# The last attention pair's steps ahead of the output gate, and half of the gate between that pair's keys and queries

## The chip, the cores and the metric

One core of one Trainium2 chip runs the kernel. The metric is the device time of one execution in microseconds, the median of three runs. Engines are named as in the profile: PE (matmul), PEld (its weight load), DVE, ACT, POOL, and SP, which here only issues DMAs.

## What is computed

One layer on 1024 tokens of width 1024, in float32. The reference, cut to what matters here:

```python
xn = rms_norm(h, attn_norm[l])
u = xn @ w_in[l]
o_a = hgrn2_mixer(u[..., o0:o1], u[..., o1:o2], u[..., o2:o3], u[..., o3:o4], lb_all[l], hg_norm[l])
o_b = fox_mixer(u[..., o4:o5], u[..., o5:o6], u[..., o6:o7], u[..., o7:IN_COLS], fox_f_bias[l], fox_norm[l])
h = h + jnp.concatenate([o_a, o_b], axis=-1) @ w_out[l]
h = h + hier_moe(rms_norm(h, ffn_norm[l]), w_group[l], b_group[l], w_expert[l], b_expert[l],
                 w_gate[l], w_up[l], w_down[l])
```

`hgrn2_mixer` is a gated recurrence over four heads of 128. Its fourth argument is the output gate: the recurrence's result is multiplied by silu of it. `fox_mixer` is causal softmax attention over eight heads of 64, with a forget bias. `hier_moe` sends every token to two of 16 experts.

## The kernel before

Each float32 operand of a large matmul is held as a rounded part (`hi`) and a remainder (`lo`), and a product is three matmuls in a row (`mm3`, lines 249 to 251). `piece` (line 168) loads one piece of a weight matrix by a DMA of SP, rounds it on ACT (line 178) and forms the remainder on DVE (line 179). The rounded pieces have three buffers.

The first half of the program is a list of calls (lines 575 to 600), one for each projection and mixer:

- `hg_fq(h)` projects forget gate and query of recurrence head h; `hg_core(h)` runs the head. Its scores are a chain of seven rounds: 16 small matmuls (line 504) into one PSUM bank (`hc`), a masked copy on DVE (lines 507 and 517), products into the query tile on DVE (lines 508 and 521) and into the key tile on POOL (line 522), then the next round. Two halves of state and output follow (lines 531 to 566).
- `fox_kq(p)` projects keys and queries of a pair of attention heads. The results leave PSUM (two banks `bk`) through ACT and DVE (lines 304 to 312) and are copied to the other 64 partitions by DMAs of SP (`mv`, line 293). Each of the two projections is 48 matmuls of 512 columns.
- `fox_core(p)` runs the pair in steps (`fox_steps`, line 352). `row` makes the logits of one block of 128 queries for one head on PE (lines 379 to 383), adds the bias and takes the minimum on DVE (line 384) and the exponential on ACT (line 388). `attend` takes two finished rows piece by piece: up to four transposes on PE (line 401), rounding on ACT (`ph`, line 406), remainder on DVE (`pl`, line 407), and matmuls with the values into one bank (`ub`, lines 411 and 412). For block pair I of 0 to 3 and either head it has I+1 pieces. `collect` copies the bank out (line 432), transposes it (line 435) and sums (line 437); after I = 1 and I = 3 `finish` normalizes and stores. The logits' tiles have four buffers.
- `hg_g(p)` projects half of the output gate: 8 token tiles of 24 matmuls of 256 columns, so 192 matmuls, each tile leaving through ACT and DVE (lines 571 and 572) and a DMA into `g_d` (line 573).

No engine's order is written out by hand. The build's scheduler places every instruction; calls that come earlier in the program go first, and later work fills in where an earlier call has nothing ready.

At the end of this half the program before mixes calls by hand. The last pair's steps are made with `steps = fox_steps(3)`: 18 of them come between `hg_g(0)` and `hg_g(1)`, and the others between the roundings of the output matrix's eight rows (`prep`, line 619: a cast on ACT at line 621, a subtraction on POOL or, for rows 2 and 5, on DVE at line 622), the first two token tiles' inputs of the output projection (`front_a`, line 629: a product with the gate on DVE at line 636, eight transposes at line 642, lines 645 and 646) and the first tile's output projection (`front_parts(0)`, line 655, 48 matmuls of 512 columns). `tc.issue_after` holds a cast of `prep` behind the latest rounding of `attend`, and a part of the projection behind the latest transposes:

```python
    def prep(k, lim=True):
        with (tc.issue_after(LF['act'].ins) if lim else nullcontext()):
            A.copy(WOH[k], raws[k])
        (G, V)[k in (2, 5)].tensor_sub(WOL[k], raws[k], WOH[k].bitcast(F32))
```

After it come the other seven tiles of the output projection with routing, and then the experts, which the change leaves alone.

Of the kernel before, what the change touches and what calls it, by code (L numbers as in the profile page):

```python
# [80 lines left out]
def build(ctx, tc, x, attn_norm, w_in, hg_lb_logits, hg_norm, fox_f_bias, fox_norm, w_out, ffn_norm,  # L81
          w_group, b_group, w_expert, b_expert, w_gate, w_up, w_down, final_norm, cf, ci, cl0, out, dbg=None):
    nc = tc.nc
    V, A, G, T = nc.vector, nc.scalar, nc.gpsimd, nc.tensor
# [12 lines left out]
    def bank():  # L97
        return ps.tile([128, 512], F32, name="bk", tag="bk", bufs=NB["bk"])
# [58 lines left out]
    def rtile(name):  # L157
        return up.tile([128, S], F32R, name=name, tag="u", bufs=NU)
# [9 lines left out]
    def piece(ks, c0, n, extra=None, raw=None):  # L168
        m = ks.stop - ks.start
        raw = wp.tile([128, m, n], F32, name="wraw", tag="wraw", bufs=1) if raw is None else raw  # L170
        hi = wp.tile([128, m, n], F32R, name="whi", tag="whi", bufs=3)
        lo = wp.tile([128, m, n], F32R, name="wlo", tag="wlo", bufs=3)
        if extra is None:
            nc.sync.dma_start(raw, w_in_v[:, ks, c0:c0 + n])
        else:
            nc.sync.dma_start(raw[:, :, 0:n - 8], w_in_v[:, ks, c0:c0 + n - 8])
            nc.sync.dma_start(raw[:, :, n - 8:n], w_in_v[:, ks, extra:extra + 8])
        A.copy(hi, raw)  # L178
        V.tensor_sub(lo, raw, hi.bitcast(F32))  # L179
        return hi, lo  # L180
# [67 lines left out]
    def mm3(o, l, r, first, last):  # L248
        T.matmul(o, l[0], r[0], start=first, stop=False)  # L249
        T.matmul(o, l[0], r[1], start=False, stop=False)  # L250
        T.matmul(o, l[1], r[0], start=False, stop=last)  # L251

    def proj_c(c0, evac):
        hi, lo = piece(slice(0, KD), c0, 128)
        for th in range(2):
            b = bank()
            t = slice(th * 512, th * 512 + 512)
            for k in range(KD):
                mm3(b, (hi[:, k], lo[:, k]), (XH[th][:, k], XL[th][:, k]), k == 0, k == KD - 1)
            evac(b, t)  # L260

    def proj_t(c0, n, evac, extra=None, pc=None):
        pc = pc or [piece(slice(4 * g, 4 * g + 4), c0, n, extra) for g in range(2)]
        for i in range(NT):
            b = bank()
            t = slice(i % 4 * 128, i % 4 * 128 + 128)
            for k in range(KD):
                hi, lo = pc[k // 4]
                mm3(b[:, :n], (XH[i // 4][:, k, t], XL[i // 4][:, k, t]), (hi[:, k % 4], lo[:, k % 4]), k == 0, k == KD - 1)
            evac(b, i)  # L270
# [22 lines left out]
    def mv(d, o):  # L293
        nc.sync.dma_start(d.bitcast(F32), o.bitcast(F32))

    def fox_kq(p):
        ka, kb, qa, qb, ql, qm = (rtile(n) for n in ("ka", "kb", "qa", "qb", "ql", "qm"))
        kl = up.tile([128, S], F32R, name="kl", tag="L", bufs=4)

        lo_, up_ = slice(0, 64), slice(64, 128)  # L300

        def ev_k(b, sl):
            for hi, h, o in ((ka, lo_, up_), (kb, up_, lo_)):
                A.copy(hi[h, sl], b[h])
                V.tensor_sub(kl[h, sl], b[h], hi[h, sl].bitcast(F32))  # L305
                mv(hi[o, sl], kl[h, sl])

        def ev_q(b, sl):
            for hi, lo, h, o in ((qa, ql, lo_, up_), (qb, qm, up_, lo_)):
                A.activation(hi[h, sl], b[h], AF.Copy, scale=-0.125)  # L310
                mv(hi[o, sl], hi[h, sl])
                V.scalar_tensor_tensor(lo[h, sl], b[h], -0.125, hi[h, sl].bitcast(F32), op0=OP.mult, op1=OP.subtract)
                mv(lo[o, sl], lo[h, sl])
        proj_c(2560 + 128 * p, ev_k)
        proj_c(2048 + 128 * p, ev_q)
        out = (((qa, ka), (ql, ka)), ((qb, kb), (qm, kb)))
        FS[p] = out
# [32 lines left out]
    LF = {}  # L350
# [107 lines left out]
    def fox_core(p):  # L458
        for _ in fox_steps(p):
            pass  # L460
# [13 lines left out]
    def hg_fq(h):  # L474
        F, K, Q = utile("hF"), utile("hK"), utile("hQ")
        HF[h], HK[h], HQ[h] = F, K, Q

        def ev_f(b, sl):
            A.activation(F[:, sl], b, AF.Tanh, scale=0.5)
            G.tensor_scalar(F[:, sl], F[:, sl], lb[:, 1, h:h + 1], lb[:, 0, h:h + 1], op0=OP.mult, op1=OP.add)  # L480
            G.tensor_scalar(K[:, sl], F[:, sl], -0.5, 0.5, op0=OP.mult, op1=OP.add)

        def ev_q(b, sl):
            A.activation(Q[:, sl], b, AF.Tanh, scale=0.5)
            V.scalar_tensor_tensor(Q[:, sl], Q[:, sl], 1.0, b, op0=OP.add, op1=OP.mult)

        proj_c(512 + 128 * h, ev_f)
        proj_c(128 * h, ev_q)
# [79 lines left out]
    def hg_g(p):  # L568
        def ev(b, i):
            z = up.tile([128, 256], F32, name="sg", tag="sg", bufs=2)  # L570
            A.activation(z, b[:, 0:256], AF.Tanh, scale=0.5)
            V.scalar_tensor_tensor(z, z, 1.0, b[:, 0:256], op0=OP.add, op1=OP.mult)
            nc.sync.dma_start(g_d[i * 128:(i + 1) * 128, 256 * p:256 * p + 256], z)
        proj_t(1536 + 256 * p, 256, ev)
# [4 lines left out]
    fox_v(0)  # L579
    fox_gate()  # L580
    fox_kq(0)
    fox_core(0)
    hg_fq(1)
    hg_core(1)
    hg_fq(2)
    fox_kq(1)
    fox_core(1)
    hg_v(1)
    hg_core(2)
    fox_v(1)  # L590
    fox_kq(2)
    fox_core(2)
    hg_fq(3)
    fox_kq(3)
    hg_core(3)
    hg_g(0)
    steps = fox_steps(3)
    for _ in range(18):
        next(steps, None)
    hg_g(1)  # L600
    w_out_v = w_out.rearrange("l (k p) c -> p (l k) c", p=128)
    raws = []
# [8 lines left out]
    WOH, WOL = [], []  # L611
# [4 lines left out]
            WOH.append(wh_[:, k])  # L616
            WOL.append(wl_[:, k])

    def prep(k, lim=True):
        with (tc.issue_after(LF['act'].ins) if lim else nullcontext()):  # L620
            A.copy(WOH[k], raws[k])
        (G, V)[k in (2, 5)].tensor_sub(WOL[k], raws[k], WOH[k].bitcast(F32))

    oa_cm = tc.tile_pool(name="oa", bufs=2, reuse_waits="tile")
# [30 lines left out]
    def front_parts(i):  # L655
        ht = HE[i] if i in HE else hp[0].tile([128, D], F32, name="ht", bufs=3)
        HT[i] = ht
        nc.sync.dma_start(ht, x2[i * 128:(i + 1) * 128, :])
        ohi, olo = OT[i]
        for c in range(2):  # L660
            b = bank()
            cs = slice(c * 512, c * 512 + 512)
            for k in range(KD):
                mm3(b, (ohi[:, k], olo[:, k]), (WOH[k][:, cs], WOL[k][:, cs]), k == 0, k == KD - 1)
                yield
            V.tensor_add(ht[:, cs], b, ht[:, cs])
        nc.sync.dma_start(h_d[i * 128:(i + 1) * 128, :], ht)

    def front_b(i):
        for _ in front_parts(i):  # L670
            pass

    next(steps, None)
    next(steps, None)
    prep(0)
    next(steps, None)
    next(steps, None)
    prep(1)
    next(steps, None)
    prep(2)  # L680
    next(steps, None)
    next(steps, None)
    prep(3)
    next(steps, None)
    front_a(0)
    front_a(1)
    prep(4)
    next(steps, None)
    next(steps, None)
    prep(5)  # L690
    next(steps, None)
    prep(6)
    next(steps, None)
    next(steps, None)
    prep(7)
    next(steps, None)
    next(steps, None)
    next(steps, None)
    fr0 = front_parts(0)
    with tc.issue_after(LF['tr'].ins):  # L700
        for _ in range(3):
            next(fr0, None)
    next(steps, None)
    with tc.issue_after(LF['tr'].ins):
        for _ in range(3):
            next(fr0, None)
    next(steps, None)
    with tc.issue_after(LF['tr'].ins):
        for _ in range(3):
            next(fr0, None)  # L710
    for _ in steps:
        pass
    for _ in fr0:
        pass
    ps_cm.__exit__(None, None, None)
    ps_cm = tc.tile_pool(name="pt", bufs=1, space=PSUM, reuse_waits="tile")
    ps = ps_cm.__enter__()
# [636 lines left out]
```

## Time and profile before

| | us |
|---|---|
| median of 3 runs | 1112.72 (1109.21 to 1117.45) |
| the profiled execution | 1116.4 |
| its span, first to last instruction | 1114.6 |
| PE busy | 1050.8 (94%) |
| DVE busy | 684.8 |
| ACT busy | 499.5 |

A timeline row gives start, duration, engine, line, operation, output tile, input tiles, shapes and count; in brackets stands the engine's idle time before it and what ended it. A row of a table by stretches gives the stretch's length, the busy time of PE, PEld, DVE, ACT and POOL in it, then PE's granted clock (1.00 is 2.4 GHz, 0.50 is 1.2 GHz), the DMA share and GB/s. Times count from the span's start. Matmul ends are modelled and matmuls overlap, so distances between starts are safer than durations.

### The profile page before, as it was taken

To read this page: it belongs to the slowest core of one execution; us is meant where nothing else is said; L and a number is where in the kernel's file an instruction comes from. 1 tells how busy PE (TensorE), PEld (TensorE's weight loads), DVE (VectorE), ACT (ScalarE), POOL (GpSimd) and SP (SyncE) were. 2 spreads that over 40 slices of the span, in tenths; PEclk is the share of its full clock that TensorE was granted. 3 is DMA by queue.
4 is the path that set the end of the run, shared out by engine and by line. 5 is a ranking of instruction groups with operands and counts; after the bars stand their busy time and mean duration, and the time that the engine had idled before them with its cause. 6 is when DMAs were issued, how large, how long until landed. Compare 5 with 4: busy or idle time off the path is not lost. (4 is left out here: it accounts for less than half of the span.)

```text
span 1114.6 us, 19354 instructions
## 1 busy us (share of the span) xinstructions
PE 1050.8 (94%) x7471; PEld 891.2 (80%) x7471; DVE 684.8 (61%) x1616; ACT 499.5 (45%) x861; POOL 366.9 (33%) x283
## 2 busy tenths in 40 slices
PE   6999999989999999899899899699999999999994
PEld 6989788869988887789777788576777778878793
DVE  4537546655575546844654576656778778777445
ACT  5423343324443333424441233465666667667341
POOL 2024123221032112410322233334655456545312
PEclk8999999989999998999979999699999999999998
DMA  7120611112121410281307942369989999999974
GB/s 243 39 58 21 151 41 48 58 38 76 31 66 30 123 48 20 62 250 40 122 30 235 361 167 76 120 225 374 370 315 329 347 322 377 298 319 374 305 285 167
DMA packets 103967, 193.98 MB, mean 174 GB/s; under 512 B 9852, under 2 KB 43756, under 8 KB 103872
## 3 DMA queue, kind: packets, MB, share of 16 engines
q1 hardware_dynamic: 92576, 169.98, 43.9%
q0 software_dynamic: 7568, 20.96, 7.5%
q10 hardware_dynamic: 3728, 1.77, 0.6%
q8 instruction: 60, 0.98, 0.4%
q14 instruction: 35, 0.29, 0.1%
HBM read 155.85 MB, written 30.68 MB: 167 GB/s over the span
## 5 line engine op out<-in xcount | busy, mean ns | idle before, releaser
L249 PE MATMUL bk<-whi,xhi 128*128 128x256 f32 (+1 forms) x384 | 112.3, 292 | 4.0 <-ACT whi L178 2.8
L1053 DVE TENSOR_TENSOR wl<-we,wh 128x1024 fp32r<-128x1024 f32 x64 | 91.9, 1445 | 35.7 <-ACT wh L1051 34.9
L251 PE MATMUL bk<-whi,xlo 128*128 128x256 f32 (+1 forms) x384 | 110.6, 288 | 0.2 <-DVE xlo L216 0.2
L250 PE MATMUL bk<-wlo,xhi 128*128 128x256 f32 (+1 forms) x384 | 109.5, 285 | 1.1 <-DVE wlo L179 1.1
L250 PE MATMUL ch<-wl,xh 128*128 128x512 f32 (+1 forms) x336 | 109.4, 326 | 0.0
L1051 ACT CAST wh<-wm 128x1024 fp32r<-128x1024 f32 x84 | 87.3, 1049 | 48.3 <-PE ch L251 45.4
L251 PE MATMUL ch<-wh,xl 128*128 128x512 f32 (+1 forms) x336 | 108.3, 324 | 0.0
L249 PE MATMUL ch<-wh,xh 128*128 128x512 f32 (+1 forms) x336 | 108.2, 329 | 0.0
L249 PE MATMUL bk<-xhi,whi 128*128 128x512 f32 x256 | 104.0, 406 | 2.6 <-DVE kl L305 2.4
L1051 ACT CAST wh<-we 128x1024 fp32r<-128x1024 f32 x84 | 87.2, 1049 | 41.2 <-PE ch L251 41.0
L1053 DVE TENSOR_TENSOR wl<-wm,wh 128x1024 fp32r<-128x1024 f32 x63 | 92.9, 1504 | 17.4 <-ACT wh L1051 17.4
L251 PE MATMUL bk<-xhi,wlo 128*128 128x512 f32 x256 | 103.4, 404 | 0.0
L250 PE MATMUL bk<-xlo,whi 128*128 128x512 f32 x256 | 102.8, 401 | 0.0
L249 PEld LDWEIGHTS bk<-whi,xhi 128*128 128x128 f32 x384 | 73.1, 190 | 5.7 <-ACT whi L178 3.1
L406 ACT CAST ph<-ch 128x512 fp32r<-128x512 f32 (+1 forms) x80 | 43.1, 542 | 75.9 <-PE ch L401 75.7
L1053 POOL TENSOR_TENSOR wl<-we,wh 128x1024 fp32r<-128x1024 f32 x20 | 51.1, 2553 | 73.7 <-ACT wh L1051 73.7
L250 PEld LDWEIGHTS bk<-wlo,xhi 128*128 128x128 f32 x384 | 73.4, 191 | 1.8 <-DVE wlo L179 1.6
L251 PEld LDWEIGHTS bk<-whi,xlo 128*128 128x128 f32 x384 | 73.3, 191 | 0.7 <-DVE xlo L216 0.4
L250 PEld LDWEIGHTS ch<-wl,xh 128*128 128x128 f32 x336 | 64.9, 193 | 9.1 <-issue 4.1
L249 PEld LDWEIGHTS ch<-wh,xh 128*128 128x128 f32 x336 | 64.5, 194 | 8.0 <-ACT xh L1065 1.6
L407 DVE TENSOR_TENSOR pl<-ch,ph 128x512 fp32r<-128x512 f32 (+1 forms) x80 | 50.3, 633 | 33.3 <-ACT ph L406 33.2
L1053 POOL TENSOR_TENSOR wl<-wm,wh 128x1024 fp32r<-128x1024 f32 x21 | 52.0, 2476 | 53.7 <-ACT wh L1051 53.6
(423 smaller groups left out, 2639.6 us busy)
## 6 DMA issues: line engine op xcount, KB each, us to landing
we<-in_w_gate_dram SPq DMA_DIRECT2D x8, 2048.0 KB, 20.0
we<-in_w_up_dram SPq DMA_DIRECT2D x8, 2048.0 KB, 18.3
we<-in_w_down_dram SPq DMA_DIRECT2D x8, 2048.0 KB, 17.9
wm<-in_w_gate_dram SPq DMA_DIRECT2D x8, 2048.0 KB, 8.3
wm<-in_w_up_dram SPq DMA_DIRECT2D x8, 2048.0 KB, 10.9
wm<-in_w_down_dram SPq DMA_DIRECT2D x8, 2048.0 KB, 14.7
wraw<-in_w_in_dram SPq DMA_DIRECT2D x26, 512.0 KB, 4.3
xt<-in_x_dram SPq DMA_DIRECT2D x8, 512.0 KB, 14.8
```

The source lines that it names most:

```text
L249: T.matmul(o, l[0], r[0], start=first, stop=False)
L250: T.matmul(o, l[0], r[1], start=False, stop=False)
L251: T.matmul(o, l[1], r[0], start=False, stop=last)
L406: LF['act'] = A.copy(ph[:, :o], b[:, :o])
L407: V.tensor_sub(pl[:, :o], b[:, :o], ph[:, :o].bitcast(F32))
L1051: A.copy(hi, src)
L1053: (G if j % 3 == 2 else V).tensor_sub(lo, src, hi.bitcast(F32))
```

## The change

`fox_kq` takes a second argument, and with it runs a half of the gate between its two projections. The last recurrence head's core goes ahead of the last pair's projections; `fox_core(3)` runs as a whole ahead of `hg_g(1)`; `prep` loses its hold; the eight roundings, two `front_a` and the first output projection follow in plain order.

```diff
-    def fox_kq(p):
+    def fox_kq(p, between=None):
...
         proj_c(2560 + 128 * p, ev_k)
+        if between is not None:
+            hg_g(between)
         proj_c(2048 + 128 * p, ev_q)
...
     hg_fq(3)
-    fox_kq(3)
     hg_core(3)
-    hg_g(0)
-    steps = fox_steps(3)
-    for _ in range(18):
-        next(steps, None)
+    fox_kq(3, 0)
+    fox_core(3)
     hg_g(1)
...
-    def prep(k, lim=True):
-        with (tc.issue_after(LF['act'].ins) if lim else nullcontext()):
-            A.copy(WOH[k], raws[k])
+    def prep(k):
+        A.copy(WOH[k], raws[k])
         (G, V)[k in (2, 5)].tensor_sub(WOL[k], raws[k], WOH[k].bitcast(F32))
...
-    next(steps, None)
-    next(steps, None)
-    prep(0)
...
+    for k in range(8):
+        prep(k)
     front_a(0)
     front_a(1)
-    prep(4)
...
-    fr0 = front_parts(0)
-    with tc.issue_after(LF['tr'].ins):
-        for _ in range(3):
-            next(fr0, None)
...
-    for _ in steps:
-        pass
-    for _ in fr0:
-        pass
+    front_b(0)
```

Lines from 296 on move by two in the program after, up to the list of calls. Up to the middle of the third pair's attention the instructions of every engine keep their order. Three places show what moves.

The first is DVE at that point, where the last recurrence head's chain begins; `sc` and `hQ` are its score and query tiles, `wlo` a weight remainder, `OF` the attention's output. Before:

```order
L407 TENSOR_TENSOR pl<-ch,ph 128x384
L179 TENSOR_TENSOR wlo<-wraw,whi 128x1024
L437 TENSOR_REDUCE OF<-ch 128x2x64 x2
L507 TENSOR_TENSOR sc<-hc,cft 128x8x64
L508 TENSOR_TENSOR hQ<-hQ,hF 128x1024
```

And now:

```order
L409 TENSOR_TENSOR pl<-ch,ph 128x384
L509 TENSOR_TENSOR sc<-hc,cft 128x8x64
L510 TENSOR_TENSOR hQ<-hQ,hF 128x1024
L439 TENSOR_REDUCE OF<-ch 128x2x64 x2
L386 ISA Lg,mn<-rb,Gt 128x512
```

The chain's first two operations now stand ahead of the sum of the attention's second block pair, and the weight remainder has gone several rows back.

The second is PE at the end of the third pair's attention, at its last `collect` (`ch<-cft,ut`). Before:

```order
L412 MATMUL ub<-pl,fv 128x128
L435 MATMUL ch<-cft,ut 128x128 x4
L554 MATMUL hc<-hv,sc 128x128 x2
L556 MATMUL hc<-st,hQ 128x128
L554 MATMUL hc<-hv,sc 128x128
L556 MATMUL hc<-st,hQ 128x128
L554 MATMUL hc<-hv,sc 128x128
L556 MATMUL hc<-st,hQ 128x128
L531 MATMUL hc<-cft,hK 128x128 x4
L249 MATMUL bk<-xhi_73,whi 128x512
L250 MATMUL bk<-xlo_74,whi 128x512
```

And now:

```order
L414 MATMUL ub<-pl,fv 128x128
L437 MATMUL ch<-cft,ut 128x128 x4
L556 MATMUL hc<-hv,sc 128x128
L558 MATMUL hc<-st,hQ 128x128
L556 MATMUL hc<-hv,sc 128x128
L558 MATMUL hc<-st,hQ 128x128
L556 MATMUL hc<-hv,sc 128x128
L558 MATMUL hc<-st,hQ 128x128
L556 MATMUL hc<-hv,sc 128x128
L558 MATMUL hc<-st,hQ 128x128
L249 MATMUL bk<-whi,xhi_73 128x256
L250 MATMUL bk<-wlo,xhi_73 128x256
```

Here the recurrence's first half stood before, and its second half came after the queries; now the second half stands here and the recurrence is done. What follows is not the queries (512 columns) but the gate's first half (256 columns): its 192 matmuls in a row, then the 48 of the queries, and then the last pair's steps with the gate's second half in between.

The third is ACT at the last token tile of the gate (the last row with `sg`). Before:

```order
L571 ACTIVATE sg<-bk 128x256
L406 CAST ph<-ch 128x512
L621 CAST wohi_5704<-woraw 128x1024
L406 CAST ph<-ch 128x384
L621 CAST wohi_5704<-woraw 128x1024 x2
L406 CAST ph<-ch 128x512
L388 ACTIVATE Lg,fls<-Lg,mn 128x896
```

And now:

```order
L573 ACTIVATE sg<-bk 128x256
L619 CAST wohi_5969<-woraw 128x1024 x4
L619 CAST wohi_5971<-woraw 128x1024 x2
L390 ACTIVATE Lg,fls<-Lg,mn 128x640
L408 CAST ph<-ch 128x512
L619 CAST wohi_5971<-woraw 128x1024 x2
L408 CAST ph<-ch 128x384
```

The eight casts of the output matrix stood singly or by twos between the attention's roundings; now six stand in a block ahead of an exponential and a rounding of the attention, and two behind these. On PE the last pair's remaining steps then run without projection matmuls between them, and the 48 matmuls of the first output projection stand behind the last `collect` and behind the transposes of the second token tile's input.

## Rows read from the trace of the kernel before

**Rows 1.** Busy time by stretch: PE, PEld, DVE, ACT, POOL, then clock.

```profile
428.16:471.74 43.58, 37.19 (x396) 31.67 (x392) 39.77 (x87) 18.31 (x35) 19.71 (x21) 0.92 0.16 48
471.74:545.00 73.26, 72.05 (x557) 69.25 (x557) 34.73 (x125) 24.35 (x56) 7.64 (x8) 1.00 0.42 126
545.00:574.70 29.70, 22.24 (x122) 18.80 (x120) 23.29 (x39) 20.57 (x32) 13.55 (x6) 0.77 0.35 111
574.70:589.50 14.80, 14.46 (x78) 12.01 (x76) 3.80 (x7) 2.24 (x4) 0.66 (x1) 1.00 0.09 27
```

**Rows 2.** Timeline of DVE where the last recurrence head's chain begins.

```profile
428.26 1.23 DVE L179 TENSOR_TENSOR wlo<-wraw,whi 128x1024 fp32r<-128x1024 f32 x1 [6.32 <-ACT whi L178]
...
430.07 0.68 DVE L507 TENSOR_TENSOR sc<-hc,cft 128x512 f32<-128x512 f32 x1
430.67 1.78 DVE L508 TENSOR_TENSOR hQ<-hQ,hF 128x1024 f32<-128x1024 f32 x1
```

**Rows 3.** Timeline of PE: first query matmul, the recurrence's second half, a wait.

```profile
471.74 0.50 PE L249 MATMUL bk<-xhi,whi 128*128 128x512 f32 x1 [0.68 <-DVE kl L305]
...
482.84 0.83 PE L538 MATMUL hc<-hv,hK 128*128 128x128 f32 x6
483.42 0.48 PE L379 MATMUL rb<-ka,qa 128*128 128x128 f32 x2
...
486.97 0.43 PE L554 MATMUL hc<-hv,sc 128*128 128x128 f32 x2
...
488.72 0.31 PE L379 MATMUL rb<-kb,qb 128*128 128x128 f32 x1
...
499.77 0.39 PE L411 MATMUL ub<-ph,fv 128*128 128x256 f32 x1 [1.21 <-ACT ph L406]
```

**Rows 4.** Timeline of ACT from the gate's last tile on, and two later roundings.

```profile
545.02 0.38 ACT L571 ACTIVATE sg<-bk 128x256 f32<-128x256 f32 x1 [2.18 <-PE bk L251]
545.63 0.59 ACT L406 CAST ph<-ch 128x512 fp32r<-128x512 f32 x1 [0.23 <-PE ch L401]
546.11 1.05 ACT L621 CAST wohi<-woraw 128x1024 fp32r<-128x1024 f32 x1
...
549.83 1.05 ACT L388 ACTIVATE Lg<-Lg,mn 128x896 f32<-128x896 f32 x1
...
573.82 0.59 ACT L406 CAST ph<-ch 128x512 fp32r<-128x512 f32 x1 [0.55 <-PE ch L401]
574.98 0.59 ACT L406 CAST ph<-ch 128x512 fp32r<-128x512 f32 x1 [0.57 <-PE ch L401]
```

**Rows 5.** Timeline of PE in the last pair's remaining steps and behind them.

```profile
552.55 1.09 PE L642 MATMUL bk<-cft,om 128*128 128x128 f32 x8 [2.61 <-DVE om L636]
...
566.04 1.11 PE L435 MATMUL ch<-cft,ut 128*128 128x128 f32 x4 [0.72 <-ACT ut L432]
...
589.51 0.50 PE L249 MATMUL bk<-wohi,ohi 128*128 128x512 f32 x1 [0.35 <-DVE he L666]
```

**Rows 6.** Timeline of DVE and of POOL: subtractions of the output matrix.

```profile
553.03 2.89 DVE L622 TENSOR_TENSOR wolo<-woraw,wohi 128x1024 fp32r<-128x1024 f32 x1
...
563.76 1.21 DVE L622 TENSOR_TENSOR wolo<-woraw,wohi 128x1024 fp32r<-128x1024 f32 x1
...
552.47 2.37 POOL L622 TENSOR_TENSOR wolo<-woraw,wohi 128x1024 fp32r<-128x1024 f32 x1 [0.52 <-ACT wohi L621]
...
569.71 2.38 POOL L622 TENSOR_TENSOR wolo<-woraw,wohi 128x1024 fp32r<-128x1024 f32 x1 [7.49 <-ACT wohi L621]
```

**Rows 7.** Timeline of DVE and POOL behind the steps: sum, product, squares.

```profile
589.37 0.75 DVE L437 TENSOR_REDUCE OF<-ch 128x128 f32<-128x256 f32 x2
...
600.35 0.69 DVE L636 TENSOR_TENSOR om<-om,gm 128x512 f32<-128x512 f32 x1 [5.57 <-DMA gm<-g_d]
...
590.26 1.04 POOL L419 TENSOR_TENSOR fsq<-OF 128x512 f32<-128x512 f32 x1 [14.90 <-DVE OF L437]
```

**Rows 8.** Busy time in the part of the steps at a lower granted clock.

```profile
559.00:571.00 12.00, 9.90 (x38) 8.13 (x38) 9.69 (x20) 7.76 (x12) 3.66 (x2) 0.50 0.20 66
```

More of the change, by code (lines that the diff above doesn't have):

```diff
@@ L671, in front_b @@
             pass
-    next(steps, None)
-    next(steps, None)
-    prep(0)
[L676 to L684, printed above, removed]
+    for k in range(8):
+        prep(k)
     front_a(0)
     front_a(1)
-    prep(4)
[L688 to L698, printed above, removed]
-    fr0 = front_parts(0)
-    with tc.issue_after(LF['tr'].ins):
-        for _ in range(3):
-            next(fr0, None)
[L703 to L710, printed above, removed]
-    for _ in steps:
-        pass
-    for _ in fr0:
-        pass
+    front_b(0)
     ps_cm.__exit__(None, None, None)
```

## Prediction

> **What bounds the kernel now.** I read the table by stretches first, then the timeline of PE for its waits in the stretches that the change touches, then ACT, DVE and POOL beside each wait. The table [rows 1] splits the touched part in four. From 428.16 (the third pair's second collect) to 471.74 (the first matmul of the fourth pair's queries [rows 3]) DVE works 39.77 of 43.58 us and PE 37.19, so DVE is the fullest and PE waits 6.4. From there to 545.00, where the gate's last matmul ends, PE works 72.05 of 73.26: a matmul less or more there is time. From 545.00 to 574.70, the last pair's remaining steps, no engine is full (PE 22.24, DVE 23.29, ACT 20.57 of 29.70): a chain from engine to engine sets the pace, and the clock is 0.77 in the mean, 0.50 for 12 us of it [rows 8]. From 574.70 to 589.50 PE is full again, with the first output projection between the steps. At 589.51 the second tile's projection begins [rows 5]. From there on both programs do the same work (seven tiles, routing, experts), and I take it as unchanged. So only 428 to 589.5 is worked out: A to 471.74, B to 545.00, C the tail of 44.5 us (29.70 and 14.80).
>
> **A: the earlier start of the last recurrence head.** DVE waits 6.32 us for a rounding ahead of 428.26 and only then does L507 (0.68) and L508 (1.78) [rows 2], on which the chain of seven rounds hangs. The order now puts these two ahead of the sum of the second block pair, in that wait. If their inputs are there, 0.68 + 1.78 = 2.46 leave the fullest engine's work behind 428 and go into the hole. Bound on the good side: the whole hole, 6.3. Bound on the bad side: more of the chain is drawn into this stretch and competes with the attention's copies; DVE has 43.58 - 39.77 = 3.8 to spare there, and filling them by work that the path does not need costs at most those 3.8. I take -2.5, what the rows price directly; nothing here needs a DMA in SP's queue to move.
>
> **B: queries, gate, steps.** The matmuls are the same ones: 48 of queries, 384 of the gate in all. The new place of the gate's first half is not a cover for the end of the third pair's attention: by the order its 192 matmuls begin only behind the last collect and the recurrence, since both banks it could use hold keys until their remainders have left. So it is a swap: queries behind it instead of ahead, and the last pair's steps have 192 gate matmuls beside them instead of 384.
> The recurrence's second half stood in the full stretch: 483.42 - 482.84 = 0.58 for its state and 488.72 - 486.97 = 1.75 for its output [rows 3]. It now stands ahead of the third pair's last collect, where PE waits anyway: -2.3. A wait of 1.21 at 499.77 [rows 3] stood where PE began the gate among the steps; with 192 matmuls done ahead, I count it gone: -1.2. Against this, the gate's weights are now rounded ahead of the queries' copies on ACT, and the queries' copies to the other partitions by SP's queue come later against the first rows that need them. I price that at +0.5; its bounds are 0 and 1.7 (a rounding of 1.05 and one of 0.59 [rows 4] in front of the copies). B is -3.0. The cover for the steps from 192 gate matmuls lasts 192/384 as long; what is late next is the tail, which therefore starts with more steps to go.
>
> **C: the tail.** Counted from the gate's last matmul.
> Before, ACT does the gate's tanh (0.38) and the next rounding of the attention ends at 546.2, 1.2 behind [rows 4]. Now six casts of 1.05 stand between, and an exponential: 0.38 + 6.3 + up to 1.05 + 0.59 = 8.3. So the attention's pieces begin 7 late. But that does not make the tail 7 longer up to the I = 2 collect. ACT's whole list to there is now 8 casts (8.4), five exponentials (5.2), five roundings (3.0), the bank's copy and the tanh (1.0), 17.6; with a wait of 0.55 for transposes at each of six [rows 4] 20.9. Before, that collect stands at 566.04 [rows 5], 21.0 behind the last gate matmul. I take no difference there.
> Behind it come the eight pieces of the last block pair. Undisturbed they pass in 1.16 each (574.98 - 573.82 [rows 4]): 9.3. Tile 0's input is rounded among them and the bank copied at their end: 1.5 and 0.6. Then four transposes, at most 1.1, half of it at full clock: 0.6. The sum 20.9 + 9.3 + 1.5 + 0.6 + 0.6 = 32.9. Before, this same end was covered by projection matmuls.
> Now the order sets the second tile's transposes ahead of the first projection on PE, and its gate product on DVE behind the sums: 0.75 for the sums, 1.04 for the squares on POOL, 0.7 for their sum (taken as the product), 0.69 for the product [rows 7], 1.09 for the transposes [rows 5]. That is 4.3, and 37.2 in all. Nothing hides it: PE's next work is queued behind those transposes.
> Then the first projection, uncovered: 48 matmuls of 512 columns, as long as the queries, 482.84 - 471.74 = 11.1 [rows 3]: 48.3.
> Clock: before, 12.00 us ran at 0.50, the lower level of 1.2 GHz, with 9.90 of matmuls that would be 5 at the upper one [rows 8]. The tail now has longer waits and no projection between the steps, so I add 3; bounds are 0 (no cold part) and 10 (two parts such as that one, each 9.90 - 4.95 = 5 longer than at full clock). The tail is 51.3 against 44.5, +6.8. Its other bounds: 2 less if the pieces overlap the rounding of tile 0, 4 more if the casts hold POOL's subtractions and with them the attention's rows.
> The subtractions of rows 2 and 5 on DVE took 2.89 beside POOL's at 552.47 and 1.21 at 563.76, where POOL was idle (its wait of 7.49 ends at 569.71) [rows 6]. Both stand under the six casts now, so neither is on the sum's path. The Trainium skill (GPSIMD Engine Reference, 1. Specifications) says that GpSimd's interfaces to SBUF are shared with VectorE, with contention for a DVE instruction that has two SBUF inputs; these rows agree. By that rule both would cost 2.89, by the row of an idle POOL 1.21; the difference of 3.4 lies in the casts' shade either way, which is inside the 4 above.
>
> **Sum.** -2.5 - 3.0 + 6.8 = +1.3 on the profiled execution's 1116.4, so 1117.7. That execution lies 3.7 over the median of 1112.7, which gives 1114.0.
>
> **The rivals.** *The tail runs cold throughout (slower).* If PE drops to 1.2 GHz in the first long wait under the six casts and stays there to the end of the first projection, every matmul of the tail doubles. Its steps are (22.24 - 9.90) + 9.90/2 + (14.46 - 11.1) = 20.7 of PE work at full clock [rows 1, 3, 8]; I put 4.2 of it into the first 8.3 us, half of them. The 16.5 left take 33.0; with 4.3 for the sums and the product and a projection of 14.8 (a third of it cold) the tail is 60.4, +15.9 against before; less 5.5 from A and B +10.4, so 1123.1. For it: 12 us at 0.50 [rows 8], in the part with the waits of 2.61 [rows 5]. Against it: the pace behind the collect at 566.04 recovered without projection matmuls. It decides if the mean clock from the last gate matmul to the last collect is under 0.6 (before, 0.77 to 574.70). The Trainium skill (TensorE: Matmul & The Clock Gate, HAM oscillation) tells of waits between short bursts that throttle the array again, each burst starting cold; the 0.50 of rows 8 agrees, and by that rule the tail would be this one.
> *The chain gains all that it can (faster).* The hole of 6.3 is won whole, B gives its 2.3 + 1.2 with nothing against it, and the tail costs 48.3 - 2 - 44.5 = 1.8, with no cold part and tile 0's rounding beside the pieces: -8.0, so 1104.7. For it: DVE is the fullest of its stretch [rows 1] and the chain is a single thread. Against it: behind 428 DVE has the attention's own work, which the earlier chain does not shorten.
> *The change does not do what it says.* The gate was to stand between keys and queries and cover something; if the engines' sums per stretch come out as before and the tail's casts fall into idle time, nothing moves: 1112.7. For it: the banks hold the gate back. Against it: the projection is uncovered by order.
>
> **How the numbers follow.** Forecast 0.64, its own range 1107 to 1121; cold tail 0.20; faster 0.11; nothing moves 0.05. The range of 8 in 10 reaches on the slow side over the cold tail (1123.1) with the upper ends of B and C, to 1127, on the fast side to 1103, under the second rival. One per cent, 11.1 us, is about what a measurement of this kernel can tell from no change: 1101.6 and 1123.8. Faster by more needs the second rival and more, half of its 0.11 and a little of the forecast's tail: 0.08. Slower by more is half of the cold tail and what is worse than it, with a part of the forecast's upper end: 0.18. Within 0.74.
>
> **What would show it.** Right: DVE's L507 ends ahead of the second block pair's sum, and the hole of 6.3 is at most 4; the queries' first matmul comes behind 192 gate matmuls in a row; from the last gate matmul to the I = 2 collect about 21 us, to the last collect about 33, to the first projection about 37, and 11 for the projection. Wrong: a hole that only moves within the attention (A falls), a first row of the last pair that waits for SP's copies by more than 1.7 (B falls), a clock under 0.6 in the tail, or a second tile's input that reaches PE before the last sums (C falls).

## The result and the profile after

The changed kernel takes 1120.06 us (median of 9 runs, 1118.13 to 1125.11), the kernel before in runs beside it 1111.66 (9 runs, 1108.67 to 1117.45). The ratio is 1.0085 with a 95% interval of 1.0067 to 1.0103: slower by 0.85%, about 9 us. The forecast was +1.3 us, inside 1%.

The profiled executions of the two differ by far less, 1116.4 and 1118.1 us, because the first profile of before was one of its slower executions. A second profile of it (run e1 below) took 1106.14 us. So three profiles are read here. The page of the changed kernel says in its first part that the engines have as much to do as before (of before PE had 1050.8, DVE 684.8, ACT 499.5):

```profile
PE 1047.4 (94%) x7471; PEld 887.4 (79%) x7471; DVE 678.5 (61%) x1616; ACT 499.2 (45%) x861; POOL 367.1 (33%) x283
```

What changed is when. The table by stretches has the same marks for each profile: the third pair's second collect, the first matmul behind that attention's end, the gate's last matmul, the I = 2 collect, the last collect, the first matmul of the second tile's projection, and the start of the experts' part. The columns are those of [rows 1]. The kernel after:

```profile
427.23:469.79 42.56, 35.97 (x395) 31.79 (x391) 37.93 (x98) 20.03 (x36) 21.06 (x22) 1.00 0.16 49
469.79:538.46 68.67, 68.67 (x529) 66.12 (x530) 28.76 (x95) 21.22 (x50) 5.83 (x7) 1.00 0.43 132
538.46:565.94 27.48, 15.49 (x69) 11.44 (x66) 23.76 (x44) 16.18 (x25) 15.01 (x7) 0.69 0.16 58
565.94:580.58 14.64, 11.80 (x75) 10.37 (x75) 7.76 (x16) 7.15 (x13) 0.00 (x0) 0.88 0.32 90
580.58:602.24 21.66, 17.51 (x76) 14.35 (x77) 8.05 (x28) 1.85 (x3) 3.12 (x4) 0.76 0.68 205
602.24:716.93 114.69, 109.90 (x619) 94.59 (x617) 68.05 (x376) 40.40 (x79) 33.84 (x24) 0.98 0.53 188
```

The kernel before in its second profile:

```profile
426.37:469.03 42.66, 34.88 (x395) 29.27 (x391) 39.51 (x87) 18.29 (x35) 18.92 (x21) 1.00 0.16 49
469.03:541.10 72.07, 72.03 (x557) 69.23 (x557) 34.72 (x125) 24.34 (x56) 7.62 (x8) 1.00 0.40 128
541.10:559.08 17.98, 12.93 (x79) 10.60 (x77) 15.73 (x27) 14.70 (x23) 10.92 (x4) 0.90 0.50 158
559.08:581.59 22.51, 22.00 (x115) 19.19 (x115) 8.52 (x17) 8.10 (x13) 4.76 (x2) 0.85 0.10 36
581.59:582.53 0.94, 0.60 (x5) 0.36 (x3) 0.74 (x2) 0.00 (x0) 0.00 (x0) 1.00 0.16 60
582.53:705.79 123.26, 114.08 (x632) 97.59 (x632) 80.37 (x399) 40.70 (x79) 37.55 (x28) 0.96 0.58 204
```

Row by row, after minus before: -0.1, -3.4, +9.5, -7.9, +20.7, -8.6, in all +10.3. Three of these say what happened. The way from the gate's last matmul to the I = 2 collect is 9.5 longer, with PE busy 15.49 of 27.48 and the clock at 0.69. In the first profile of before it took 21.04 (566.04 - 545.00), so against that one it is 6.4 longer. The first projection, which before lay between the pieces (the -7.9 is its absence there), now stands alone behind the last collect, with a wait: +20.7. And 8.6 come back in the other tiles' projections.

What holds up the first of these shows on DVE. Its timeline in that stretch (in line numbers of the program after; `rsqrt` is lines 115 to 121, here on 128x8):

```profile
540.16 2.14 DVE L115 TENSOR_SCALAR fls<-fls 128x8 f32<-128x8 f32 x1
542.22 0.16 DVE L116 TENSOR_SCALAR fls<-fls 128x8 int32<-128x8 int32 x1
542.29 0.47 DVE L386 CUSTOM_DVE_ANT_0 Lg<-rb,Gt,mn 128x256 f32<-128x256 f32 x1
...
542.70 1.95 DVE L117 TENSOR_SCALAR fls<-fls 128x8 int32<-128x8 int32 x1
544.67 2.27 DVE L119 TENSOR_TENSOR fls<-fls 128x8 f32<-128x8 f32 x1
...
547.48 1.80 DVE L120 TENSOR_TENSOR fls<-fls 128x8 f32<-128x8 f32 x1
549.20 3.43 DVE L620 TENSOR_TENSOR wolo<-woraw,wohi 128x1024 fp32r<-128x1024 f32 x1
...
553.78 0.15 DVE L119 TENSOR_TENSOR fls<-fls 128x8 f32<-128x8 f32 x1
```

Four operations on 128x8 (L115, L117, L119, L120) take 1.80 to 2.27 us each; L119, done once more at 553.78 with POOL idle, takes 0.15. POOL meanwhile, and what PE waits for (two rows of its timeline):

```profile
539.90 11.65 POOL L620 TENSOR_TENSOR wolo<-woraw,wohi 128x1024 fp32r<-128x1024 f32 x5 [1.64 <-ACT wohi L619]
```

```profile
547.61 0.79 PE L381 MATMUL rb<-ka,qa 128*128 128x512 f32 x1 [4.10 <-DVE mn L386]
...
553.22 0.79 PE L381 MATMUL rb<-ka,qa 128*128 128x512 f32 x1 [4.39 <-DVE mn L386]
```

Five subtractions in a row, 2.33 each in the mean, end at about 542.2, 544.6, 546.9, 549.2 and 551.55. The four slow DVE operations end at 542.30, 544.65, 546.94 and 549.28, and the subtraction of 3.43 at 552.63, so it lost its first 2.3. Each waits for the end of the POOL instruction that it finds running. L116, which starts at 542.22 between two of them, takes 0.16. The row's minimum (L386, logits from PSUM with a bias from SBUF) is not stretched, 0.47, but it is queued behind the others, and PE waits for it.

The second, behind the last collect, on PE and DVE:

```profile
580.58 0.66 PE L437 MATMUL ch<-cft,ut 128*128 128x128 f32 x4 [0.68 <-ACT ut L434]
584.67 1.97 PE L640 MATMUL bk<-cft,om 128*128 128x128 f32 x8 [3.44 <-DVE om L634]
587.35 0.80 PE L249 MATMUL bk<-wohi,ohi 128*128 128x512 f32 x1 [0.71 <-DVE olo L644]
```

```profile
583.33 0.69 DVE L422 TENSOR_REDUCE fls<-fsq 128x8 f32<-128x512 f32 x1 [1.30 <-POOL fsq L421]
583.93 0.68 DVE L634 TENSOR_TENSOR om<-om,gm 128x512 f32<-128x512 f32 x1
```

The second tile's product comes behind the last sums, and its transposes hold the projection, as the order had it. The transposes take 1.97 for the 1.09 of [rows 5], and the projection's first matmul 0.80 for 0.50: the clock is at its lower level there (0.60 in the mean from 580.58 to 587.35).

### The profile page after: what moved, and what is told of

Read it like the earlier page. It is cut to its first block, busy times and chain, and to the rows that moved or that the text cites. A ratio compares the mean times of both kernels' runs of the same rounds, so it can differ in the third digit from the quotient of the medians.

```text
span 1116.3 us, 19349 instructions
## 1 busy us (share of the span) xinstructions
PE 1047.4 (94%) x7471; PEld 887.4 (79%) x7471; DVE 678.5 (61%) x1616; ACT 499.2 (45%) x861; POOL 367.1 (33%) x283
## 5 line engine op out<-in xcount | busy, mean ns | idle before, releaser
L390 ACT ACTIVATE Lg<-Lg,mn 128x128 f32<-128x128 f32 (+3 forms) x64 | 49.7, 777 | 53.9 <-DVE mn L386 44.7
```

Of the source, the lines that this page charges most:

```text
L390: A.activation(L[:, :nb * 128], L[:, :nb * 128], AF.Exp, scale=-1.0, bias=prev, accum_out=fl[:, 0, i, hh:hh + 1])
```

## Experiments

The theories ("us under the changed kernel" is a difference of medians that were not taken side by side; the ratios are to the kernel before, run beside each). Theory P: POOL's subtractions, now in a block, hold DVE's small operations and so PE (from the gate's last matmul to the I = 2 collect). Theory G: the second tile's gate product is late and uncovers the first projection. Rivals: the six casts on ACT set the stretch; what the tail loses is won back behind it and costs nothing; the executions scatter by as much.

**e1: the kernel before once more.** No edit.

> The kernel before, a second profile, to see how far the parts differ between two executions. Counted from the third pair's second collect: start of the queries 471.7, last gate matmul 545.0, second tile's projection 589.5, first matmul of line 915 at 713.6, end 1114.6 were the first profile's. If the two profiles agree to 1 us up to 589.5 and differ behind 713.6 by several us, the part of the change's +8.4 us that its own profile does not show (+1.7) is scatter of the experts' part; if they differ in 589.5 to 713.6, the 8 us that the changed kernel seems to win back there is scatter.

The run took 1106.14 us. From the second collect to the start of the queries it is 42.66, against 43.58 in the first profile [rows 1], which had a granted clock of 0.92 there (1.00 here); to the I = 2 collect from there 90.05 against 94.30; the experts' part 398.5 against 401.0. So two executions of one kernel differ by 10 us, 6.0 of it between the second collect and the experts' part; 4.0 of these lie in two stretches in which the first one had the lower clock (0.92 against 1.00 to the queries, 0.82 against 0.90 from the gate's last matmul to the I = 2 collect). The 8.6 that the changed kernel wins back is no scatter: 123.3 and 124.1 (713.60 - 589.51) in the two profiles of before.

**e2: all subtractions on DVE.**

```diff
-        (G, V)[k in (2, 5)].tensor_sub(WOL[k], raws[k], WOH[k].bitcast(F32))
+        V.tensor_sub(WOL[k], raws[k], WOH[k].bitcast(F32))
```

> The changed kernel with all eight subtractions of the output matrix on DVE, none on POOL. Theory 1 (small DVE operations with both inputs in SBUF wait for the end of POOL's subtraction): the square root's operations of lines 115 to 120 go from 1.8-2.3 us back to 0.15-0.2, PE's waits of 4.10 and 4.39 us for the row's minimum fall under 2, and the way from the last gate matmul to the I=2 collect goes from 27.5 to 19-22 us although DVE gets 6 x 1.2 = 7 us more to do; time about 5 us under the changed kernel, 1115. Theory 2 (the six casts on ACT set the tail): ACT's list is the same, so the way stays 26-28 us and the time 1118-1122, or gets longer by the added 7 us of DVE work.

Median 1113.62, ratio to before 1.0025 (1.0007 to 1.0043): 6.4 us under the changed kernel. The same operations of its DVE timeline:

```profile
541.85 0.17 DVE L115 TENSOR_SCALAR fls<-fls 128x8 f32<-128x8 f32 x1
...
545.29 0.17 DVE L117 TENSOR_SCALAR fls<-fls 128x8 int32<-128x8 int32 x1
...
549.30 0.16 DVE L119 TENSOR_TENSOR fls<-fls 128x8 f32<-128x8 f32 x1
```

And its stretch from the gate's last matmul to the I = 2 collect:

```profile
539.02:560.93 21.91, 15.60 (x68) 12.62 (x65) 20.32 (x49) 16.08 (x25) 1.04 (x1) 0.69 0.10 34
```

21.91 for 27.48, with the same casts on ACT (16.08 busy) and six more subtractions on DVE, whose busy time yet falls from 23.76 to 20.32. PE's waits for the row's minimum from the gate's last matmul to the last collect, in the changed kernel and in e2 (total, times, longest):

```profile
PE rb L381 <- DVE mn L386: 10.3, 3, 4.4
```

```profile
PE rb L381 <- DVE mn L386: 3.8, 4, 1.3
```

The long waits were POOL's doing; the casts in ACT's block stay, and the stretch is within 1.0 of the forecast's 20.9. The clock is 0.69 in either: it did not set the difference.

**e8: POOL's subtractions in halves.**

```diff
-        (G, V)[k in (2, 5)].tensor_sub(WOL[k], raws[k], WOH[k].bitcast(F32))
+        if k in (2, 5):
+            V.tensor_sub(WOL[k], raws[k], WOH[k].bitcast(F32))
+        else:
+            for c in range(2):
+                cs = slice(c * 512, c * 512 + 512)
+                G.tensor_sub(WOL[k][:, cs], raws[k][:, cs], WOH[k][:, cs].bitcast(F32))
```

> The changed kernel with each of POOL's six subtractions cut into two of 512 columns. POOL's whole work stays (11.7 us and some). Theory 1 (a DVE operation with both inputs in SBUF, or a small one in SBUF alone, waits till the running POOL instruction ends): the operations of lines 115 to 120 that took 1.8-2.3 us take 0.9 to 1.3, two pass in the time of one, PE's waits of 4.10 and 4.39 for the row's minimum fall to 2 to 2.6, last gate matmul to I=2 collect 23 to 25 instead of 27.8 us, time 2 to 4 us under the changed kernel. Theory 2 (DVE is slowed evenly by POOL's traffic while it runs): the operations stay at about 2 us each and the time stays 1119 to 1121.

Median 1117.67, ratio 1.0049 (1.0029 to 1.0068), 2.4 us under the changed kernel. DVE and POOL in the stretch:

```profile
541.75 1.05 DVE L115 TENSOR_SCALAR fls<-fls 128x8 f32<-128x8 f32 x1
...
543.19 0.86 DVE L117 TENSOR_SCALAR fls<-fls 128x8 int32<-128x8 int32 x1
544.08 1.19 DVE L119 TENSOR_TENSOR fls<-fls 128x8 f32<-128x8 f32 x1
...
545.80 0.70 DVE L120 TENSOR_TENSOR fls<-fls 128x8 f32<-128x8 f32 x1
```

```profile
541.49 14.41 POOL L625 TENSOR_TENSOR wolo<-woraw,wohi 128x512 fp32r<-128x512 f32 x10 [1.64 <-ACT wohi L619]
```

The operations are half as long because the instruction they wait for is. An even slowing by POOL's traffic would have left them near 2. PE's longest waits for the minimum fall to 1.93 and 2.23, and the stretch to 24.38 (564.43 - 540.05). POOL pays too. The mean of the ten halves is 1.44, but seen singly eight take about 1.27, and the two that find a subtraction of DVE running take 2.25 and 2.33. One of these, with DVE's subtraction, which had itself waited for the half before:

```profile
546.42 2.37 DVE L621 TENSOR_TENSOR wolo<-woraw,wohi 128x1024 fp32r<-128x1024 f32 x1
```

```profile
547.67 2.25 POOL L625 TENSOR_TENSOR wolo<-woraw,wohi 128x512 fp32r<-128x512 f32 x1
```

DVE's ends at 548.79 and POOL's 1.13 later: whichever starts second waits for the other to end.

**e4 and e6: the first projection covered, in two ways.** e4 puts it ahead of the second tile's input; e6 gives that tile's gate a large tile.

```diff
     front_a(0)
-    front_a(1)
     front_b(0)
+    front_a(1)
```

```diff
-... else ltile("gm")[:, 0:512]
+... else utile("gm")[:, 0:512]
```

> The changed kernel with the first tile's projection ahead of the second tile's input in the program; by the order 48 projection matmuls then stand between the pieces of the last block pair. Theory 1 (the last collect, the sums and the second tile's product kept PE from the projection: 580.6 to 600.7 us): the projection is covered as far as the pieces have waits, the time from last collect to the second tile's projection falls from 20 us to 9-12, the clock there rises to 0.9 or more, time 5 to 9 us under the changed kernel, 1111 to 1115. Theory 2 (what the tail loses is won back behind it, since the loads for the experts run meanwhile): the tail gets shorter by 8 us, but the output projection behind it gets longer by as much, and the time stays within 3 us of 1120.

> The changed kernel with one line different: the second token tile's gate is loaded into one of the sixteen large tiles and not into one of the four logits' tiles. By the order its product then stands on DVE before the last sums and the 48 projection matmuls between the last pieces. Theory 1 (the product waited for the logits' tile that the last row held, and the first projection for the product): last collect to the second tile's projection from 20.2 us to under 2, tail 50 to 53 instead of 62.6 us, the output projection behind it about 124 us as in the kernel before (116 in the changed one), so in all 2 to 5 us under the changed kernel, 1115 to 1118. Theory 2 (the projection behind the tail gives back all, as where it was put first): 1119 to 1121. Theory 3 (the tail's cold clock goes with the wait): 1110 to 1113.

e4: 1118.73, ratio 1.0073 (1.0049 to 1.0096), not to be told from the changed kernel, as theory 2 had it. From last collect to the second tile's projection 7.6 us (591.22 to 598.84): the projection is covered, but the second tile's product is as late as ever and now holds that tile's own projection (PE waits 3.4 for it, and 1.6 for its remainder). From the gate's last matmul to that projection it is 5.8 shorter than in the changed kernel (57.96 for 63.78), and the seven other tiles are 4.9 longer (119.61 for 114.69).

e6: 1116.74, ratio 1.0046 (1.0028 to 1.0063), 3.3 under. Last collect to second projection is 0.41 (591.06 to 591.47), against 21.66. But the pieces take 23.00 with the projection among them, against 14.64, and the seven other tiles 124.5 against 114.69: of 21.25 won, 8.4 go to the pieces and 9.8 are given back. Theory G names the wait rightly, and theory 1's time holds; the rival holds for a large part of it.

**e7: both mended** (e2's and e6's edits together).

> Both mended: second tile's gate in a tile of its own and all eight subtractions on DVE, else the changed kernel. If the two causes add (POOL's subtractions beside DVE's small operations, -6.5 us as measured with the subtractions alone; the gate's tile, -2 to -5), the time is 1107 to 1112, a ratio to the kernel before of 0.998 to 1.002. If the gate's tile alone is worth nothing, it is the 1113.6 of the subtractions alone.

1108.92, ratio 0.9979 (0.9962 to 0.9997): 11.1 under the changed kernel and a little under the kernel before. The two savings, 6.4 and 3.3, add to 9.7; with intervals of some 2 us on each, that agrees with two causes that add, and it leaves the kernel where the first half of the change alone has it (e3 below), so no loss clear of the noise is left. Its stretches:

```profile
539.22:560.89 21.67, 15.36 (x69) 12.47 (x66) 20.32 (x49) 16.09 (x25) 1.04 (x1) 0.68 0.15 45
560.89:583.29 22.40, 21.41 (x131) 18.15 (x131) 10.74 (x21) 8.71 (x15) 0.00 (x0) 1.00 0.36 115
583.29:584.14 0.85, 0.65 (x5) 0.42 (x5) 0.75 (x2) 0.00 (x0) 0.00 (x0) 1.00 0.58 125
584.14:706.81 122.67, 112.42 (x632) 96.17 (x632) 81.41 (x399) 40.61 (x79) 37.24 (x28) 0.98 0.59 207
```

With the projection among the pieces the clock is 1.00 here from the I = 2 collect to the second projection. Beside e2, which differs only in the gate's tile, one sees what is given back: e2 has 22.13 from the last collect to the second projection and 114.72 behind it.

**e3, e5 and e9: the first half of the change, whole and in parts,** each with the tail of the kernel before. e3:

```diff
-    fox_kq(3)
     hg_core(3)
-    hg_g(0)
+    fox_kq(3, 0)
     steps = fox_steps(3)
```

e5 has `hg_core(3)` ahead of `fox_kq(3)` alone, with `hg_g(0)` behind; e9 `fox_kq(3, 0)` alone, with `hg_core(3)` behind it.

> The first half of the change alone: recurrence core ahead of the last pair's projections, the gate's first half between keys and queries; the tail as in the kernel before (holds, projection between the steps). Theory 1 (the head gains 6.5 us, the tail loses it and more): last gate matmul at about 538.5 as in the changed kernel, tail 44 to 50 us instead of 62, time 4 to 6 us under the kernel before, 1106. Theory 2 (with only 192 gate matmuls beside them more steps are left for the tail, whatever its order): the tail is as long as in the changed kernel less the 15 us of uncovered sums and projection, 50 to 55, and the time is that of the kernel before within 2 us.

> The kernel before with one move alone: the last recurrence head's core ahead of the last pair's projections. The gate, the steps and the tail stay as they were. Theory 1 (the head's gain is the recurrence's second half, 0.58 + 1.75 us taken out of the full stretch, and nothing of the gate's place): the same gain as with the whole first half of the change, 3 us, so a ratio of 0.997 to the kernel before. Theory 2 (the recurrence's move only shifts waits; the gain of the first half is the gate between keys and queries): 1.000 within 0.002.

> The kernel before with the other move of the first half alone: the gate's first half between the last pair's keys and queries; the recurrence core stays behind the projections. The two moves together measured 0.9973 of the kernel before, the recurrence's alone 1.0015. Theory 1 (the gain of the first half is the gate's place): 0.996 to 0.998. Theory 2 (neither gains alone, the gate's place only with the recurrence out of the way): 0.999 to 1.003.

e3: 1108.70, ratio 0.9973 (0.9958 to 0.9989), some 3 us faster than before, less than theory 1's 4 to 6, with a tail in its range: 45.4 us (541.77 to 587.19). e5: 1113.26, 1.0015 (0.9999 to 1.0031), no gain. e9: 1108.68, 0.9986 (0.9972 to 0.9999), half of e3's gain, between its two theories, and its interval reaches e3's. So the recurrence's move alone brings nothing and the gate's alone between nothing and all. The traces speak for the two together: from the second collect to the gate's last matmul it is 114.73 us in e1, 114.96 in e5 and 114.27 in e9, and 110.98 to 112.57 in the eight profiled kernels that have both moves (111.24 in the changed kernel, 112.57 in e3). Part of this is work put off and not saved: 25 of the rows' matmuls (tile `rb`) are left behind the gate's last one, for 20 in e1. Why it takes both moves was not tested.

**e10: the tail alone.**

```diff
     hg_g(0)
-    steps = fox_steps(3)
-    for _ in range(18):
-        next(steps, None)
+    fox_core(3)
     hg_g(1)
```

with the end of the program as in the changed kernel.

> The kernel before with the new tail alone: gate and recurrence stand as before, the last pair's core runs as a whole, the eight casts without hold, then the two inputs and the first projection. Theory 1 (the tail is what costs, and its cost does not hang on where the gate's first half stands): the changed kernel's 1.0085 over the first half's 0.9973, so 1.011, with PE's waits for the row's minimum while POOL subtracts. Theory 2 (with 384 gate matmuls beside the steps fewer steps are left for the stretch in which POOL subtracts): 1.002 to 1.007, last gate matmul to I=2 collect 14 to 20 us instead of 27.8.

1114.97, ratio 1.0050 (1.0034 to 1.0067). With all 384 gate matmuls beside the steps the I = 2 collect comes 9.5 us behind the last of them (558.91 - 549.38), sooner than theory 2's 14 to 20, since most steps are done by then; the time is in its range. The parts do not add: 1.0050 times 0.9973 is 1.0023, and both together measured 1.0085. The first half takes away the work that covered the steps, and the tail puts its casts and subtractions where that cover is missing: behind the gate's last matmul e10 has 8 of the rows' matmuls left, the changed kernel 25, and in e10 PE waits there for no row's minimum, in the changed kernel 10.3 us.

**e11: the first half with the tail of before, all subtractions on DVE** (e3's and e2's edits).

> The first half of the change with the tail of the kernel before, and all eight subtractions on DVE. In that tail POOL's subtractions stand singly behind the held casts, and DVE's product and subtractions beside them took 2.77, 2.89 and 1.86 us instead of 0.7 and 1.2. Theory 1 (these stretched operations are on the tail's path): 2 to 4 us under the first half alone, 0.994 to 0.996 of the kernel before. Theory 2 (six more subtractions of 1.2 us cost DVE what the contention did): 0.997 to 0.999.

1107.93, ratio 0.9975 (0.9961 to 0.9989), the same as e3. In e3's trace DVE's products and subtractions had taken 0.69, 1.59, 1.21 and 1.43 there, so there was little to win on these. But POOL's single subtractions held two operations of the square root, L117 and L121; the first, with the POOL instruction beside it:

```profile
545.72 1.68 DVE L117 TENSOR_SCALAR fls<-fls 128x8 int32<-128x8 int32 x1
```

```profile
544.99 2.38 POOL L623 TENSOR_TENSOR wolo<-woraw,wohi 128x1024 fp32r<-128x1024 f32 x1 [2.98 <-ACT wohi L622]
```

So POOL holds DVE also when its instructions stand singly, as [rows 6] had shown. PE's waits for the row's minimum between the gate's last matmul and the last collect fall from 3.1 us in e3 (the longest 1.6) to 0.7 in e11, but this stretch takes 44.47 us in e3 and 44.31 in e11: what is won there is lost beside it, and no run shows to what. e3, e7 and e11 are each a little faster than both kernels and not to be told from one another.

## Why the prediction was near, and by what

The range of 1103 to 1127 and the case of "within 1%" hold. The sum was too small, +1.3 for some +9, and several of its steps fell; errors of both signs lay in it, so that it came so near is in part luck: a tail 11.0 us longer than forecast (62.3 for 51.3) was set off by 8.6 won back in the tiles behind it. Of the signs that it named, the order's two came: L507 (now L509) ahead of the second block pair's sum, and the queries behind the gate's 192 matmuls. The lengths did not: a hole of 6.04 for at most 4, and 27.48, 42.12, 48.89 and 13.39 for about 21, 33, 37 and 11.

- *A, -2.5: fell.* Behind the second collect it is 42.56 in the changed kernel and 42.66 in e1. The two operations went ahead of the sum, as told, and a hole stayed:

```profile
420.05 0.69 DVE L509 TENSOR_TENSOR sc<-hc,cft 128x512 f32<-128x512 f32 x1
420.66 1.22 DVE L510 TENSOR_TENSOR hQ<-hQ,hF 128x1024 f32<-128x1024 f32 x1
427.92 0.76 DVE L439 TENSOR_REDUCE OF<-ch 128x128 f32<-128x256 f32 x2 [6.04 <-PE ch L437]
```

  DVE waits 6.04 for PE's collect, and PE was busy 28.00 of the 28 us up to 428. The step that failed is "2.46 leave the fullest engine's work": DVE's work in the stretch did fall, from 39.51 to 37.93, and its length by 0.1, so DVE was the fullest but not what was waited for. The one microsecond that the first profile had more, 43.58, goes with its clock of 0.92.
- *B, -3.0: near in size by luck, wrong in its terms.* The whole first half measured 3 (1.2 to 4.7), and the stretch is 3.4 shorter (72.07 to 68.67). But the -2.3 for the recurrence's second half is not there by itself: in e5 this half has left the stretch, A is 42.57, and B is 72.39 with PE busy 70.95, so waits took the place (time +1.7, from 0 to +3.4). The wait of 1.21 [rows 3], priced at -1.2, is not in e1 (PE busy 72.03 of 72.07), so the gate's place had no such wait to win; alone it gave -1.6 (e9, from -3.1 to -0.1). Together the two moves do shorten the stretch, in part by steps left for the tail; the rest of the reason stays open.
- *C to the I = 2 collect, 20.9: the mechanism I left out.* With no subtraction on POOL the stretch is 21.91 and 21.67 (e2, e7), near the 20.9 of ACT's list; that ACT sets it there is not shown, since DVE, with six subtractions more, is fuller (20.32 against 16.08). The 5.6 above that (27.48 - 21.91) are POOL's. The prediction had the two rows [rows 6] and put the cost for both of DVE's subtractions "in the casts' shade", with a bound of 4 for the attention's rows; it did not ask which other DVE operations stand beside POOL's block. The square root of the first half (behind the I = 1 collect) did, ahead of the rows' minimum. The Trainium skill (GPSIMD Engine Reference, 1. Specifications) names contention with DVE instructions that run in a two-port mode or have two SBUF inputs. This trace agrees for the two operations with two inputs, L119 and L120, with 2.27 and 1.80 for about 0.15 on operands of eight columns. L115 and L117 have one input and were held as long (2.14 and 1.95); in which mode they run no run shows. The timeline and e8 show that the wait lasts to the end of POOL's instruction.
- *C behind it.* Eight pieces with tile 0's input and the last copy, 9.3 + 1.5 + 0.6 = 11.4, took 14.64, at a mean clock of 0.88. The last sums and the product, with the last transposes 0.6 + 4.3 = 4.9, took 6.77, at 0.60. The projection, 11.1, took 13.39 (587.35 to 600.74), at 0.82. The lump of 3 for the clock stood for these three, 7.4 in all; it was too small and inside its bounds. The tail is 62.3 against the 51.3 forecast: 6.6 + 7.4 - 3.
- *The other tiles, "taken as unchanged": fell, the other way.* 114.69 for 123.26. PE's waits there by the view of waits, the kernel before in its second profile and then the kernel after:

```profile
PE ch L849 <- DVE si L857: 2.8, 2, 1.7
PE ch L842 <- DVE mem L839: 2.2, 1, 2.2
PE ch L642 <- issue: 0.9, 1, 0.9
PE ch L642 <- DVE om L636: 0.8, 1, 0.8
PE bk L251 <- DVE olo L646: 0.6, 1, 0.6
```

```profile
PE ch L803 <- DVE mem L800: 2.2, 1, 2.2
PE ch L810 <- DVE si L818: 1.1, 1, 1.1
```

  Waits for the third tile's input (L642, L646) and half of that for the routing's slots (L849, now L810) are gone. Sixteen transposes, some 1.7 us, also lie ahead of the mark after and behind it before. That it goes with the projection's place the runs show, 114.7 to 115.0 in the four kernels that have it uncovered (after, e2, e8, e10), 119.6 to 124.5 in the nine other profiles; that the inputs load while PE is still at the uncovered projection would explain it, and was not tested by itself.
- *The rivals.* The cold tail gave 1123.1 and a tail of 60.4, near to what came, but its condition was not met: the clock from the last gate matmul to the last collect is (27.48 x 0.69 + 14.64 x 0.88) / 42.12 = 0.76, over 0.6, and e2 wins 5.6 of that stretch at the same 0.69. The faster rival failed with A. "Nothing moves" failed.

## What to carry to other kernels

Before work of POOL is gathered into a block, look at the small DVE operations that will stand beside it: each may cost as long as one POOL instruction, however few columns it has (2.27 us here for eight), single POOL instructions hold them too (1.68 and 1.98 in e3), and one of them ahead of an operation that PE waits for puts that on the path. A tile that is loaded for the next stage should not come out of a pool whose buffers the last steps of this stage hold. And take a second profile of the kernel before: a stretch's length with a dip of the clock is no measure of what a moved instruction can win.

## What the runs showed of the hardware

A DVE operation on 128x8 took up to 2.27 us beside a POOL subtraction of 2.33 and 1.19 beside one of half the columns, and 0.15 to 0.17 with POOL idle, while DVE's row minimum from PSUM kept its 0.47. The hold goes both ways: a POOL half of about 1.27 took 2.25 and 2.33 where it started within a DVE subtraction of 128x1024. An operation that starts just ahead of the other engine's is not held (L116, 0.16 at 542.22). And two executions of one kernel differed by 10 us on a single core, 1106.1 and 1116.4, of which 1.8 lay ahead of the second collect, 2.5 in the experts' part and 6.0 between, 4.0 of these in two stretches in which the slower one had the lower clock (428 to 472, 0.92 against 1.00, and the tail's first part, 0.82 against 0.90).
